# High and low parts of the normalised activations at another pair of places in most parts, in steps of 32 and 64 bytes

## The chip, the core and the metric

The kernel runs on one core of one Trainium2 chip. The metric is the device time of one execution in microseconds (us). Before the change it is 2287.13 us, the median of 3 runs (2279.85 to 2287.46).

## What is computed

The reference is a network of 4 layers over 256 tokens of 1024 features, in 32-bit floats. Each layer has three parts, each with a norm before and a norm after, so there are twelve parts, numbered 0 to 11 here (s in the code).

```python
for i in range(DEPTH):                                   # DEPTH = 4
    f = swiglu(rms_norm(x, norm_pre[i, 0]), w_gate, w_up, w_down)
    x = x + 0.5 * rms_norm(f, norm_post[i, 0])           # part 3i
    hn = rms_norm(x, norm_pre[i, 1])
    m = (dilated_attention, diff_attention, swa_sink_attention)[i % 3](hn, ...)
    x = x + rms_norm(m, norm_post[i, 1])                 # part 3i+1, "mixer"
    f = swiglu(rms_norm(x, norm_pre[i, 2]), ...)
    x = x + 0.5 * rms_norm(f, norm_post[i, 2])           # part 3i+2
```

So parts 0, 2, 3, 5, 6, 8, 9 and 11 are feed-forward parts with one shape (1024 to 2816 and back), parts 1 and 10 are the same dilated attention with other weights, part 4 is the differential attention, and part 7 the attention with a window and sinks.

## The kernel before

Every matrix product is computed as three matmuls on numbers that are split into a high and a low part: `mm3` (lines 173 to 176) issues high by high (line 174), high by low (175) and low by high (176) into one PSUM tile. The weights come from memory in units of 128x2048 numbers through `raw`; ScalarE rounds a unit to `hi` (line 141), and VectorE or GpSimd subtracts to get `lo` (line 142). `hi` and `lo` have four buffers each, and unit i, counted from the start of the program, uses buffer i mod 4. When a unit is used up, `done` starts the split of the unit four places later and a load behind that.

The normalised activations are transposed in `norm_tr_`: TensorE transposes four blocks into a PSUM bank, ScalarE rounds them into the high part of `xT` and VectorE subtracts to get the low part. `xT` is one tile of one buffer, made anew by `new_xT` at the first transposes of each part. It holds 2 x 2048 numbers and 64 more per partition; the high part begins 48 numbers (192 bytes) after the tile's start, and the low part 2048 numbers behind the high part.

In a feed-forward part (`ffn`) the first four units are used token by token: `xT` is the stationary operand, and the weights stream, 512 columns at a time, into `g` and `u` (48 matmuls each). The other 18 units are used feature by feature: the weights are stationary, and `xT` streams, 256 columns at a time, into `gu`. These are 18 x 48 = 864 matmuls in each of the eight feed-forward parts, in pairs of a gate unit and an up unit. Behind the first gate unit stand eight transposes (line 372). In the end `closing` multiplies the result, `hT`, by 11 more units, 512 columns at a time, into `acc`. A feed-forward part uses 33 units.

A mixer uses `xT` in the same two ways: as the stationary operand in the leading units (`lead`) and for the values (`v`), and streamed for the queries and keys (`qk`). Between these stand the scores (`sc`), transposes and weighted sums of the heads. Parts 1 and 10 use 44 units, part 4 uses 16 and part 7 uses 9. The result, `oT`, is multiplied in `closing` as well. `hT` and `oT` have places of their own, which the change doesn't touch.

TensorE's order is the program's order. Each matmul is a weight load (PEld in the profile) and a stream (PE); the load of the next matmul runs while the present one streams.

Of the kernel before, what the change touches and what calls it, by code (L numbers as in the profile page):

```python
# [45 lines left out]
def tile_network(  # L46
# [35 lines left out]
    def bank(tag, name):  # L82
        return ps.tile([P, 512], F32, tag=tag, name=name, bufs={"mm": 3, "s": 2, "tr": 2, "o": 1}[tag])
# [111 lines left out]
    xT = {}  # L195

    NX, NH = KD * SEQ, KF * SEQ

    def two(z, o, n):

        return [z[:, o + i * n:o + (i + 1) * n].rearrange("p (k n) -> p k n", n=SEQ) for i in range(2)]

    def new_xT():
        z = actp.tile([P, 2 * NX + 64], F32R, tag="xT", name="xT")
        xT["h"], xT["l"] = two(z, 48, NX)

    def xt(k, t):
        sl = slice(t * P, (t + 1) * P) if t is not None else slice(0, SEQ)
# [2 lines left out]
    def rstd_of(a, b, whole=False):  # L211

        ms = small.tile([P, 1], F32, tag="ms", name="ms")
        if whole:
            pool.tensor_scalar(out=ms, in0=a, scalar1=b, scalar2=None, op0=ALU.add)
        elif b is None:
            pool.tensor_scalar(out=ms, in0=a, scalar1=EPS, scalar2=None, op0=ALU.add)
        else:
            pool.tensor_scalar(out=ms, in0=a, scalar1=b, scalar2=EPS, op0=ALU.add, op1=ALU.add)  # L219
        r = small.tile([P, 1], F32, tag="rstd", name="rstd")  # L220
        state["rstd"] = pool.tensor_tensor(out=r, in0=ms, in1=half, op=ALU.pow).ins
        return r

    hn_of = {}

    def norm_elem(t, s, parts=1):

        ss = small.tile([P, 1], F32, tag="ssx", name="ssx")
        hn = actp.tile([P, D], F32, tag="w", name="hn", bufs=3)
        act.activation(out=hn, in_=x[:, t], func=AF.Square, scale=1.0 / 32.0, accum_out=ss)  # L230
        r = rstd_of(ss, None)
        state["norm"] = state["rstd"]
        for c in range(parts):
            cs = slice(c * D // parts, (c + 1) * D // parts)
            i = dve.scalar_tensor_tensor(out=hn[:, cs], in0=x[:, t, cs], scalar=r, in1=gains["pre", s][:, cs],
                                     op0=ALU.mult, op1=ALU.mult)
        hn_of[t] = hn
        return i

    def boundary_elem(t, s, acc, mid):  # L240
# [4 lines left out]
    def boundary_elem_(t, s, acc):  # L245

        ss = small.tile([P, 2], F32, tag="ssf", name="ssf")
        for i in range(2):
            act.activation(out=junk, in_=acc[i], func=AF.Square, scale=1.0 / 32.0,  # L249
                           accum_out=ss[:, i:i + 1])  # L250
        u = actp.tile([P, 2, 512], F32, tag="w", name="u", bufs=3)
        fac = 1.0 if s % 3 == 1 else 0.5
        g = gains["post", s].rearrange("p (i n) -> p i n", i=2)
        for i in range(2):
            dve.scalar_tensor_tensor(out=u[:, i], in0=acc[i], scalar=fac, in1=g[:, i],
                                     op0=ALU.mult, op1=ALU.mult)
        r = rstd_of(ss[:, 0:1], ss[:, 1:2])
        if s + 1 < 3 * DEPTH:
            dve.scalar_tensor_tensor(out=x[:, t], in0=u.rearrange("p i n -> p (i n)"), scalar=r,
                                     in1=x[:, t], op0=ALU.mult, op1=ALU.add)  # L260
            norm_elem(t, s + 1)
            return
        for i in range(2):
            cs = slice(i * 512, (i + 1) * 512)
            dve.scalar_tensor_tensor(out=x[:, t, cs], in0=u[:, i], scalar=r, in1=x[:, t, cs],
                                     op0=ALU.mult, op1=ALU.add)
            nc.sync.dma_start(out=out[:, t, cs], in_=x[:, t, cs])

    def norm_tr(t):
        with tc.high_priority(PR2) if t == 0 else ExitStack():  # L270
            return norm_tr_(t)

    def norm_tr_(t):
        hn = hn_of.pop(t)
        if t == 0:
            new_xT()
        for g in range(2):
            tp = bank("tr", "tp")
            for j in range(4):
                k = 4 * g + j  # L280
                pe.transpose(tp[:, j * P:(j + 1) * P], hn[:, k * P:(k + 1) * P], ident)
            tv = tp.rearrange("p (i n) -> p i n", i=4)
            h = xT["h"][:, 4 * g:4 * g + 4, t * P:(t + 1) * P]
            i = act.copy(out=h, in_=tv)
            dve.tensor_tensor(out=xT["l"][:, 4 * g:4 * g + 4, t * P:(t + 1) * P], in0=tv,
                              in1=h.bitcast(F32), op=ALU.subtract)
        return i
# [716 lines left out]
    if True:  # L1004
# [10 lines left out]
        with tc.high_priority(PRI):  # L1015
            i = norm_elem(0, 0, 2)
            j = norm_tr(0)
# [3 lines left out]
        with tc.issue_after(j.ins):  # L1021
            norm_elem(1, 0)
# [156 lines left out]
```

## Time and profile before

| | before |
|---|---|
| median of 3 runs | 2287.13 us |
| the profiled execution's own time | 2287.67 us |
| its span | 2285.8 us |
| TensorE, matmuls | 99% busy, 15,696 of them |
| TensorE, weight loads | 92% |
| VectorE, ScalarE, GpSimd | 55%, 52%, 28% |
| packets of the loads from memory, share of 16 DMA engines | 48.3% |

The busy time of TensorE is made of matmuls that overlap: a new one starts before the last one has drained. A matmul of 256 columns has a record of some 0.28 us, while the next starts 0.11 to 0.12 us later. So the share of busy time doesn't tell at what rate TensorE works. The rate is read from the starts in the timeline, or from the length of a stretch over the number of its matmuls.

### The profile page before, as it was taken

The page shows a single profiled execution, that of the slowest core. Times are in us where ns is not written, and L with a number is a line of the kernel's source. Part 1 is how long each engine was busy: PE and PEld are TensorE (multiplying, and loading weights), DVE is VectorE, ACT ScalarE, POOL GpSimd, SP SyncE. Part 2 cuts the span into 40 slices and gives each one's busy share as a digit, 9 for nine tenths or more (in the row PEclk, how much of TensorE's full clock was granted, in tenths as well). Part 3 has the DMA queues.
Part 4 walks back from the last instruction along what each step waited for, and adds up shares of the span by engine and source line. Part 5 has one row for each costly group of instructions (what it writes and reads, how often), then busy time and mean ns, then how long its engine had stood idle before and what let it go on. Part 6 is the DMA issues. An engine that isn't in the chain of part 4 may idle for free.

```text
span 2285.8 us, 38031 instructions
## 1 busy us (share of the span) xinstructions
PE 2253.5 (99%) x15696; PEld 2097.1 (92%) x15696; DVE 1253.8 (55%) x1814; ACT 1195.0 (52%) x2086; POOL 633.7 (28%) x640
## 2 busy tenths in 40 slices
PE   8999999999999999999999999999999999999998
PEld 7989999989989989889889987899899899998997
DVE  6555544565555555565465558654655544446653
ACT  6445666654444446654354448543444476665542
POOL 0005877620020028620020024100200287774000
PEclk9999999999999999999999999999999999999999
DMA  7554444445545545255555542555555544443552
GB/s 289 194 189 174 166 153 153 157 184 185 185 173 217 201 164 172 93 218 187 185 202 189 199 169 93 188 200 187 202 185 191 189 168 149 146 157 138 217 189 92
DMA packets 60519, 404.99 MB, mean 177 GB/s; under 512 B 6966, under 2 KB 7867, under 8 KB 16315
## 3 DMA queue, kind: packets, MB, share of 16 engines
q1 hardware_dynamic: 60202, 402.51, 48.3%
q8 instruction: 123, 2.02, 0.3%
q14 instruction: 50, 0.40, 0.1%
q10 hardware_dynamic: 144, 0.07, 0.0%
HBM read 401.50 MB, written 1.05 MB: 176 GB/s over the span
## 4 chain that ended last, share of the span: by engine, by line
PE 91%; DVE 4%; ACT 2%; POOL 2%; DMA 1%; issue 1%; SPq 0%; POOLq 0%; DVEq 0%; ACTq 0%
PE gu L175 12%; PE gu L174 12%; PE gu L176 12%; PE acc L176 8%; PE acc L174 8%; PE acc L175 8%; PE qk L174 4%; PE qk L175 4%; PE qk L176 4%; PE v L174 2%; PE v L175 2%; PE v L176 2%; PE tp L813 2%; DVE lo L142 1%; PE u L176 1%; PE u L175 1%
## 5 line engine op out<-in xcount | busy, mean ns | idle before, releaser
L141 ACT CAST hi<-raw 128x1024 fp32r<-128x1024 f32 (+2 forms) x970 | 775.1, 844 | 772.5 <-issue 492.9
L142 DVE TENSOR_TENSOR lo<-raw,hi 128x1024 fp32r<-128x1024 f32 (+1 forms) x546 | 661.6, 1250 | 422.6 <-ACT hi L141 422.2
L174 PE MATMUL gu<-xT,hi 128*128 128x256 f32 x2304 | 640.8, 278 | 0.0
L175 PE MATMUL gu<-xT,hi 128*128 128x256 f32 x2304 | 640.1, 278 | 0.0
L176 PE MATMUL gu<-xT,lo 128*128 128x256 f32 x2304 | 640.0, 278 | 0.0
L142 POOL TENSOR_TENSOR lo<-raw,hi 128x512 fp32r<-128x512 f32 (+1 forms) x424 | 546.5, 1322 | 146.3 <-ACT hi L141 146.0
L174 PEld LDWEIGHTS gu<-xT,hi 128*128 128x128 f32 x2304 | 436.0, 189 | 0.3
L175 PEld LDWEIGHTS gu<-xT,hi 128*128 128x128 f32 x2304 | 432.6, 188 | 0.4
L176 PEld LDWEIGHTS gu<-xT,lo 128*128 128x128 f32 x2304 | 432.5, 188 | 0.0
L219 POOL TENSOR_SCALAR ms<-ssf 128x1 f32<-128x1 f32 x24 | 7.2, 300 | 1393.0 <-ACT junk L249 1392.0
L176 PE MATMUL acc<-hi,hT 128*128 128x512 f32 x704 | 276.0, 392 | 0.0
L175 PE MATMUL acc<-lo,hT 128*128 128x512 f32 x704 | 275.9, 392 | 0.0
L174 PE MATMUL acc<-hi,hT 128*128 128x512 f32 x704 | 274.6, 390 | 0.0
L174 PE MATMUL qk<-xT,hi 128*128 128x256 f32 x800 | 226.1, 283 | 0.0
L176 PE MATMUL qk<-xT,lo 128*128 128x256 f32 x800 | 223.2, 279 | 0.0
L175 PE MATMUL qk<-xT,hi 128*128 128x256 f32 x800 | 223.2, 279 | 0.0
L175 PEld LDWEIGHTS acc<-lo,hT 128*128 128x128 f32 x704 | 132.2, 188 | 28.1
L176 PEld LDWEIGHTS acc<-hi,hT 128*128 128x128 f32 x704 | 132.2, 188 | 28.1
L174 PEld LDWEIGHTS acc<-hi,hT 128*128 128x128 f32 x704 | 132.3, 188 | 26.4
L174 PEld LDWEIGHTS qk<-xT,hi 128*128 128x128 f32 x800 | 151.6, 190 | 0.2
L176 PEld LDWEIGHTS qk<-xT,lo 128*128 128x128 f32 x800 | 151.0, 189 | 0.1
L175 PEld LDWEIGHTS qk<-xT,hi 128*128 128x128 f32 x800 | 150.8, 189 | 0.2
(267 smaller groups left out, 3298.2 us busy)
## 6 DMA issues: line engine op xcount, KB each, us to landing
raw<-in_w_ffn_dram SPq DMA_DIRECT2D x263, 1024.0 KB, 4.8
raw<-in_w_a_qk_dram SPq DMA_DIRECT2D x48, 1024.0 KB, 4.8
raw<-in_w_a_v_dram SPq DMA_DIRECT2D x32, 768.0 KB, 4.3
raw<-in_w_a_out_dram SPq DMA_DIRECT2D x8, 1024.0 KB, 4.8
raw<-in_w_b_qk_dram SPq DMA_DIRECT2D x8, 1024.0 KB, 5.2
gain<-in_g_pre_dram SPq DMA_DIRECT2D x12, 512.0 KB, 6.3
gain<-in_g_post_dram SPq DMA_DIRECT2D x12, 512.0 KB, 7.1
raw<-in_w_b_v_dram SPq DMA_DIRECT2D x4, 1024.0 KB, 4.7
```

The lines of the kernel that those rows point to most:

```text
L141: act.copy(out=hi[:, cs], in_=r[:, cs])
L142: eng.tensor_tensor(out=lo[:, cs], in0=r[:, cs], in1=hi[:, cs].bitcast(F32), op=ALU.subtract)
L174: pe.matmul(o, lhsT=a[0], rhs=b[0], start=first, stop=False)
L175: pe.matmul(o, lhsT=a[0], rhs=b[1], start=False, stop=False)
L176: pe.matmul(o, lhsT=a[1], rhs=b[0], start=False, stop=last)
L219: pool.tensor_scalar(out=ms, in0=a, scalar1=b, scalar2=EPS, op0=ALU.add, op1=ALU.add)
L813: pe.transpose(tp[:, c0:c0 + P], src, ident)
```

## The change

`new_xT` is told the part's number, and takes the places of the high and the low part from a table with a pair for each part. The first number of a pair is the place of the high part, in numbers of 4 bytes from the tile's start, the second that of the low part, less 2048. Before, both were 48 in all parts. Parts 0, 3 and 10 keep (48, 48). The tile has the same size and place as before, and every engine has the same instructions in the same order with the same waits; only the addresses in `xT` differ, of its two writers (ScalarE and VectorE) and its reader (TensorE).

| part | kind | high, low | in bytes, against before |
|---|---|---|---|
| 1 | mixer | 48, 64 | 0, +64 |
| 2 | feed-forward | 32, 48 | -64, 0 |
| 4 | mixer | 32, 64 | -64, +64 |
| 5 | feed-forward | 16, 48 | -128, 0 |
| 6 | feed-forward | 16, 64 | -128, +64 |
| 7 | mixer | 48, 56 | 0, +32 |
| 8 | feed-forward | 40, 48 | -32, 0 |
| 9 | feed-forward | 40, 40 | -32, -32 |
| 11 | feed-forward | 56, 56 | +32, +32 |

```diff
-    def new_xT():
+    def new_xT(s):
         z = actp.tile([P, 2 * NX + 64], F32R, tag="xT", name="xT")
-        xT["h"], xT["l"] = two(z, 48, NX)
+        a, b = ((48, 48), (48, 64), (32, 48), (48, 48), (32, 64), (16, 48), (16, 64), (48, 56), (40, 48),
+                (40, 40), (48, 48), (56, 56))[s]
+        xT["h"] = two(z, a, NX)[0]
+        xT["l"] = two(z, b, NX)[1]
...
-        hn_of[t] = hn
+        hn_of[t] = hn, s
...
-        hn = hn_of.pop(t)
+        hn, s = hn_of.pop(t)
         if t == 0:
-            new_xT()
+            new_xT(s)
```

## Rows read from the trace of the kernel before

**Rows 1.** The page: span, granted clock in 40 slices, chain by engine.

```profile
span 2285.8 us, 38031 instructions
...
PEclk9999999999999999999999999999999999999999
...
PE 91%; DVE 4%; ACT 2%; POOL 2%; DMA 1%; issue 1%; SPq 0%; POOLq 0%; DVEq 0%; ACTq 0%
```

**Rows 2.** Stretches of `gu`: from:to, length, busy (matmuls), clock, DMA share, GB/s.

```profile
36.10:135.00 98.90, 98.24 (x864) 1.00 0.57 205
500.70:603.10 102.40, 101.77 (x864) 1.00 0.54 197
687.80:786.60 98.80, 98.17 (x864) 1.00 0.56 204
1003.70:1106.10 102.40, 101.77 (x864) 1.00 0.54 196
1190.70:1289.60 98.90, 98.25 (x864) 1.00 0.56 203
1468.50:1567.30 98.80, 98.17 (x864) 1.00 0.55 203
1651.90:1754.40 102.50, 101.84 (x864) 1.00 0.54 196
2120.10:2219.00 98.90, 98.24 (x864) 1.00 0.56 205
```

**Rows 3.** Timeline of TensorE, part 3, behind the transposes: start, us, instruction.

```profile
694.03 0.37 PE L174 MATMUL gu<-xT,hi 128*128 128x256 f32 x1
...
694.47 0.28 PE L174 MATMUL gu<-xT,hi 128*128 128x256 f32 x1
...
694.92 0.28 PE L175 MATMUL gu<-xT,hi 128*128 128x256 f32 x1
```

**Rows 4.** Timeline of TensorE at the same place of part 2.

```profile
506.95 0.36 PE L174 MATMUL gu<-xT,hi 128*128 128x256 f32 x1
...
507.39 0.28 PE L174 MATMUL gu<-xT,hi 128*128 128x256 f32 x1
...
507.86 0.28 PE L175 MATMUL gu<-xT,hi 128*128 128x256 f32 x1
```

**Rows 5.** Tile views, `gu` (part 0, end of part 2), `qk` (part 1): ns min/median/max.

```profile
L175 PE MATMUL gu<-xT,hi x288: 276/276/282, 36.3 to 134.7; 128*128 128x256 f32 x144
...
L175 PE MATMUL gu<-xT,hi x10: 281/281/281, 599.7 to 602.9; 128*128 128x256 f32 x10
...
L175 PE MATMUL qk<-xT,hi x352: 276/280/282, 218.0 to 432.4; 128*128 128x256 f32 x176
```

**Rows 6.** Timeline of TensorE: `lead` of part 1, `g` and `u` of part 2.

```profile
212.26 0.28 PE L175 MATMUL lead<-lo,xT 128*128 128x256 f32 x1
...
217.21 0.28 PE L175 MATMUL lead<-lo,xT 128*128 128x256 f32 x1
...
490.40 0.39 PE L174 MATMUL g<-hi,xT 128*128 128x512 f32 x1
...
500.01 0.39 PE L174 MATMUL u<-hi,xT 128*128 128x512 f32 x1
```

**Rows 7.** Timeline of TensorE: `closing` of part 2, scores of part 1.

```profile
606.13 0.39 PE L175 MATMUL acc<-lo,hT 128*128 128x512 f32 x1
...
609.99 0.39 PE L174 MATMUL acc<-hi,hT 128*128 128x512 f32 x1
...
233.09 0.28 PE L174 MATMUL sc<-dg01h,qgh 128*128 128x256 f32 x1
...
233.45 0.28 PE L174 MATMUL qk<-xT,hi 128*128 128x256 f32 x1
```

**Rows 8.** Tile views, ScalarE: casts into `xT` and into `hT`, ns min/median/max.

```profile
L284 ACT CAST xT<-tp x48: 578/587/609, 10.9 to 2108.0; 128x512 fp32r<-128x512 f32 x48
...
L375 ACT CAST hT<-tp x16: 577/588/603, 44.1 to 2128.5; 128x512 fp32r<-128x512 f32 x16
```

## The prediction

> **What bounds the kernel now.** First the page: TensorE holds 91% of the chain of work that ended last, and its granted clock stands in the top tenth in all 40 slices [rows 1], which is the upper of its two levels, 2.4 GHz. So the end is set by the rate at which matmuls follow each other, and a gain has to come out of their spacing. Then the stretches of `gu`, the same 864 matmuls in each of eight parts. They come out at two lengths and nothing between: 98.2 us in parts 0, 3, 6, 8 and 11, and 101.8 us in parts 2, 5 and 9 [rows 2], with the same clock of 1.00 and nearly the same DMA share. Over 864 that is a spacing of 98.17 / 864 = 113.6 ns and 101.77 / 864 = 117.8 ns, 4.2 ns apart. Then the timeline at the place where the two part. Behind the eight transposes both parts begin alike, with a first matmul of 0.36 to 0.37 us and three steps that take 0.44 us in both. Then part 3 goes on with four steps in 694.92 - 694.47 = 0.45 us, or 0.113 us each [rows 3], part 2 with four in 507.86 - 507.39 = 0.47 us, or 0.118 us [rows 4], and each stays so for the rest of the stretch: the record of a matmul is 276 ns in the parts with the tight spacing and 281 ns in those with the wide one, with next to no spread [rows 5].
>
> So there are two steady spacings, tight and wide, and what starts them is small. What tells the parts apart? The instructions, waits and places of `xT` are the same in all eight. The buffers of the weights are not: a unit uses buffer i mod 4, and with 33 units in a feed-forward part and 44, 16 and 9 in the mixers the eight parts begin at units 0, 77, 110, 159, 192, 234, 267 and 344. The three that begin at an odd number, 77, 159 and 267, are parts 2, 5 and 9, those with the wide spacing: a match in eight out of eight. In these the gate units stand in the buffers where the other parts have their up units. I read this as the stream's place in SBUF against that of the weights which load meanwhile: an argument from a match, not a proof. The change moves one of the two sides.
>
> 113.6 ns looks like the floor of this operation. The closing matmuls, 512 columns on other tiles, follow at (609.99 - 606.13) / 17 = 227.1 ns [rows 7], twice 113.5, and no stretch of 256 columns that I found goes below 113 ns.
>
> **The change, term by term.** The sum is made against the profiled execution's 2287.67 us (span 2285.8 [rows 1] and 1.9 around it), which lies 0.5 above the median of 2287.13.
>
> `gu` of parts 2, 5 and 9 (moved, wide): 101.77 + 101.77 + 101.84 = 305.38 us. At the floor, with the mean of the five tight parts of 98.21, they would take 3 x 98.21 = 294.64. Between the bounds 0 and -10.74 I take **-10.7**, since the spacing that more parts show is the tight one, and the wide one has been seen in `gu` only with a pairing that goes away here.
>
> `gu` of parts 6, 8 and 11 (moved, tight): they can't fall below the floor, and can be thrown into the wide spacing, at 3 x (101.79 - 98.21) = +10.7. Between 0 and +10.7 I take **0**, by the rows they show now. Parts 0 and 3 are not moved: 0.
>
> `qk` of part 1 (1,056 matmuls; only the low part moves): a median of 280 ns on one of its lines, between the two records, with a smallest of 276 [rows 5], says that about half of them have the wide spacing. From half to none is 1,056 x 0.5 x 4.2 ns = -2.2 us; if three quarters of the matmuls have it and all lose it, -3.3; if the tight half turns wide, +2.2. I take **-2.2**, by the same reasoning as for `gu`. The few `qk` of parts 4 and 7 go with the next term.
>
> Token by token, where `xT` is the load and the weights stream: `g` and `u` in six moved parts (576), `lead` in parts 1, 4 and 7 (536) and `v` in parts 1 and 4 (480). `lead` runs at (217.21 - 212.26) / 42 = 117.9 ns and `g` and `u` at (500.01 - 490.40) / 42 = 228.8 ns [rows 6]. Against 113.6 and 227.1 that leaves at most 536 x 4.3 + 576 x 1.7 + 480 x 4.3 (`v` priced as `lead`) = 5.3 us. The other way, the widest steady spacing at hand, 0.36 / 3 = 120 ns in the scores [rows 7], would cost 1,592 x 2.1 ns = +3.3. I take a third of the gain, **-1.8**, since no second level is seen there.
>
> The writers of `xT`: the casts take a median of 587 ns into `xT`, and 588 ns into `hT` from the same bank, at another place [rows 8]. So a place costs them nothing, and 48 of them would be 0.5 us at 10 ns each: **0**. If TensorE takes less time, the loads and splits behind it must keep up: the tight parts already live with that at 0.55 to 0.57 of the DMA engines [rows 2], so nothing new is late.
>
> Sum: 2287.67 - 10.7 - 2.2 - 1.8 = **2273.0 us**.
>
> **A rule that speaks against it.** Two spacings of one instruction stream stand in the stretches of `gu` [rows 2], and they differ by what is read from where. The Trainium skill, "SBUF — State Buffer", section "Who interferes with whom", says that TensorE has two read ports of its own, for the stream and for the weights, and never waits on anyone; its specifications put the lines of SBUF at 16 bytes, so that steps of 32 and 64 bytes leave a stream's place in a line as it was. By that page no place is better than another, and the sum would be 2287 us. The trace doesn't settle it, since no run here has `xT` elsewhere; but a rule by which places are all alike has no room for the odd and the even parts.
>
> **The rivals.** (1) A new draw: the place decides, but as by lot. Five of eight parts are tight now. Drawn so, the three wide parts gain 3 x 5/8 x 3.6 = 6.7 us and the three tight ones lose 3 x 3/8 x 3.6 = 4.0, net -2.7; with half of the smaller terms (-2.0) that is 2283 us, anywhere from 2276 to 2290. For it: mixers, with many restarts, mix both records in one line [rows 5]. Against: a new place was hardly needed where a part is tight. (2) Nothing happens: the spacing is set by the timing behind the transposes and not by the place, and the change does nothing that can be measured: 2287 us. For it: the two entries differ by hundredths of a us [rows 3, 4]. Against: the odd and even units. The page of the Trainium skill named above would give this time for another reason. (3) Slower than before: the new places throw the quick `gu` of parts 6, 8 and 11 into the wide spacing, while parts 2, 5 and 9 keep theirs, as a larger distance to the weights' buffers makes the streams meet more often. The price is +10.7, and with the token-by-token matmuls at 120 ns (+3.3) the time is 2301.7 us. It decides from the point where two more parts are lost than won. For it: `lead` reads the same two tiles in exchanged roles and shows the wide spacing alone [rows 6]. Against: five tight parts out of eight.
>
> **How the numbers follow.** My forecast has a chance of 0.55, rival 1 has 0.25, rival 2 has 0.13 and rival 3 has 0.07. About 0.5%, 11.4 us, is what a measurement of this kernel can tell from no change; so under 2275.7 is faster and over 2298.6 slower. The forecast lies on the faster side by 2.7 us only: a little of it (two of three wide parts won) falls to the same, and rival 1 gives as much back at its good end. So faster 0.55, same 0.38, slower 0.07. The range: all bounds on the good side give 2287.67 - 10.7 - 3.3 - 5.3 = 2268.4, and one of the runs before lies 7.3 below the median, twice 3.6, as if two parts had changed their spacing in it; I go to 2264. On the other side it takes in rivals 1 and 2, to 2288. Left out are rival 3 and the ends, under 0.2 in all.
>
> **What would show it.** The stretches of `gu` in parts 2, 5 and 9 at 98.2 us and not 101.8 prove the main term; each that stays costs 3.6. The same stretches in parts 6, 8 and 11 at 98.2 prove the second, at 101.8 rival 3. `qk` of part 1 with a median of 276 to 277 on all three lines proves the third, and `lead` under 117.9 or `u` under 228.8 the fourth. All eight stretches as before would be rival 2. Parts 0, 3 and 10, not moved, must stay; if part 3 or 10 changes, timing has a hand in it. A spacing under 113 ns would show that my floor is none, and the time could then fall below the range.

## The result: 2307.86 us, slower by 0.9%

The changed kernel takes 2307.86 us, the median of 4 runs (2305.27 to 2313.5), against 2287.3 us before (4 runs). The ratio is 1.0091, with a 95% interval of 1.0073 to 1.0109. I had forecast 2273.0 us, a gain of 0.6%, with a range of 2264 to 2288. The time lies 20 us above the range and on the other side of no change.

The page of the changed kernel shows the same picture as before: the same instructions, TensorE at the head of the chain, the clock at its upper level.

```profile
span 2307.1 us, 38031 instructions
...
PEclk9999999999999999999999999999999999999999
...
PE 90%; DVE 4%; POOL 3%; ACT 2%; DMA 1%; issue 1%; SPq 0%; POOLq 0%; DVEq 0%; ACTq 0%
```

The stretches of `gu`, in the order of parts 0, 2, 3, 5, 6, 8, 9, 11 (columns as in [rows 2]):

```profile
35.70:134.50 98.80, 98.16 (x864) 1.00 0.57 204
503.80:609.30 105.50, 104.83 (x864) 1.00 0.53 191
693.90:792.80 98.90, 98.25 (x864) 1.00 0.56 203
1009.90:1112.60 102.70, 102.05 (x864) 1.00 0.55 196
1197.40:1301.00 103.60, 102.94 (x864) 1.00 0.53 193
1480.10:1582.80 102.70, 102.05 (x864) 1.00 0.54 196
1667.70:1771.10 103.40, 102.77 (x864) 1.00 0.53 194
2137.20:2240.30 103.10, 102.47 (x864) 1.00 0.54 196
```

Put beside [rows 2], parts 0 and 3, which are not moved, stand at 98.2 us as before. All six moved parts lie at 102 us or over: part 6 rose by 4.7 us, 8 by 3.9, 11 by 4.2, and of the three that I had hoped to win back part 2 rose by 3.1, 5 by 0.3 and 9 by 0.9. The sum is +17.1 us of the 21.3 by which the span grew. `qk` of part 1 (all 1,056 matmuls) now takes 132.80 us, against 129.96 before, while part 10 with the same shape and the old pair takes 129.96 in both kernels. In order: part 1 before, part 1 after, part 10 after:

```profile
195.00:477.60 282.60, 129.96 (x1056) 1.00 0.44 159
...
195.00:480.40 285.40, 132.80 (x1056) 1.00 0.43 157
...
1831.00:2113.70 282.70, 129.96 (x1056) 1.00 0.45 159
```

In that stretch of part 1 no line of `qk` reaches the record of 276 ns any more, which was the smallest in [rows 5], and the median is 281 ns on all three. One of them (ns min/median/max):

```profile
L175 PE MATMUL qk<-xT,hi x352: 277/281/285, 217.6 to 435.0; 128*128 128x256 f32 x176
```

Token by token, `g` and `u` of part 2 follow at (497.08 - 494.74) / 10 = 234 ns, against 228.8 in [rows 6]:

```profile
494.74 0.40 PE L174 MATMUL g<-hi,xT 128*128 128x512 f32 x1
...
497.08 0.39 PE L175 MATMUL g<-lo,xT 128*128 128x512 f32 x1
```

So 17.1 us are from `gu`, 2.8 from `qk` of part 1, and most of the rest from `g` and `u`. In these stretches TensorE doesn't sit idle: each matmul of a moved part follows its predecessor by a few ns more.

How far the spacing went is seen best behind the transposes. The 80 us from 1020 to 1100 lie there in part 5 in both kernels; the first line is before, the second after:

```profile
1020.00:1100.00 80.00, 80.00 (x682) 1.00 0.53 186
...
1020.00:1100.00 80.00, 80.00 (x682) 1.00 0.52 185
```

The same 682 matmuls: part 5 goes on at the wide spacing that it had, 117.8 ns, and most of its 0.3 us more lies in the unit ahead of the transposes, which was tight before. Part 8 fell from the tight spacing to this same wide one. The other four moved parts are wider still, from 118.3 ns in part 11 to 121 in part 2.

### The profile page after: what moved, and what is told of

It reads as the page before. It is cut to its first block, busy times and chain, and to the rows that moved or that the text cites. A ratio compares the mean times of both kernels' runs of the same rounds, so it can differ in the third digit from the quotient of the medians.

```text
span 2307.1 us, 38031 instructions
## 1 busy us (share of the span) xinstructions
PE 2275.5 (99%) x15696; PEld 2117.3 (92%) x15696; DVE 1252.6 (54%) x1814; ACT 1194.4 (52%) x2086; POOL 633.0 (27%) x640
## 4 chain that ended last, share of the span: by engine, by line
PE 90%; DVE 4%; POOL 3%; ACT 2%; DMA 1%; issue 1%; SPq 0%; POOLq 0%; DVEq 0%; ACTq 0%
PE gu L175 12%; PE gu L176 12%; PE gu L174 12%; PE acc L174 8%; PE acc L176 8%; PE acc L175 7%; PE qk L174 4%; PE qk L175 4%; PE qk L176 4%; PE v L176 2%; PE v L175 2%; PE v L174 2%; POOL lo L142 2%; PE tp L816 1%; PE u L176 1%; PE u L174 1%
```

## The experiments

Three things had to be told apart: whether the place or the entry sets the spacing, against what the place counts, and whether anything moved can reach the tight spacing. All kernels compute the whole network. Each was timed and traced in one execution, except where a median is given. The fences of this section show stretches of `gu`, with the columns of [rows 2].

**Three parts back.** The changed kernel's table with three pairs undone:

```diff
-        ... (16, 48), (16, 64), (48, 56), (40, 48), (40, 40), (48, 48), (56, 56))[s]
+        ... (16, 48), (48, 48), (48, 56), (48, 48), (40, 40), (48, 48), (48, 48))[s]
```

> The changed kernel, with parts 6, 8 and 11 put back to the pair (48, 48). Theory A, the spacing of a part's matmuls is set by the places of its own xT against the buffers of the weights: the three stretches of gu go from 102.9, 102.1 and 102.5 us back to 98.2, the other parts stay to 0.1 us (part 2 at 104.8, part 9 at 102.8), and with the token-by-token matmuls (some 0.5 us a part) the time is 2309 - 13 - 1.5 = 2294.5 us. Theory B, the spacing is set by the timing with which a stretch is entered: parts that are not edited here change as well, by 3.6 us or more each, and the sum does not come out.

It took 2297.61 us, 3 us over the sum of theory A. Parts 2, 6, 8 and 11:

```profile
505.00:607.90 102.90, 102.13 (x864) 1.00 0.55 195
1195.70:1294.80 99.10, 98.35 (x864) 1.00 0.58 203
1473.40:1576.00 102.60, 101.88 (x864) 1.00 0.55 196
2130.00:2229.00 99.00, 98.27 (x864) 1.00 0.58 203
```

Parts 6 and 11 came back, as A says. Part 8 came back to (48, 48) and to its other spacing, the wide one that it did not have before. And part 2, which was not edited here, fell from 104.8 to 102.1 us. So neither theory does alone: the pair sets which spacings a part can have, and something else picks one of them.

**The buffers of the weights turned.** One buffer is passed over at the start, all pairs (48, 48):

```diff
+        if i == 0:
+            for tag in ("hi", "lo"):
+                z = wp.tile([P, 2048], F32R, tag=tag, name=tag)
+                pool.memset(z[:, :1].bitcast(F32), 0.0)
         hi = wp.tile([P, 2048], F32R, tag="hi", name="hi")
```

> The kernel before, with one set of the weights' four buffers passed over at the start, so that every unit of weights stands one buffer further; all pairs (48, 48). Theory A, in the form that the match of odd and even units suggests (which buffer a unit stands in matters): the stretches of gu of parts 2, 5 and 9 go from 101.8 to 98.2 us, and those of parts 0, 3, 6, 8 and 11 from 98.2 to 101.8, +7.2 us in all, 2295 us. Theory B (timing at the entry): no swap, the eight stretches stay as they are or change without a pattern. If only the place within 256 bytes counts, the buffers are alike, nothing changes, and the time is 2287 us.

It took 2285.01 us. Parts 2, 5, 6 and 9:

```profile
501.40:600.50 99.10, 98.37 (x864) 1.00 0.57 203
...
1000.80:1099.90 99.10, 98.37 (x864) 1.00 0.57 203
1184.20:1286.80 102.60, 101.87 (x864) 1.00 0.55 196
...
1649.20:1751.80 102.60, 101.90 (x864) 1.00 0.55 197
```

No swap: parts 6 and 9 are wide, all others tight. The match of odd units and wide parts, on which I had built, does not hold.

**Before, once more.** The same program in another execution.

> The kernel before once more, in an execution of its own. If the entry timing picks between the two spacings that (48, 48) allows, and differs from execution to execution, other parts than 2, 5 and 9 lie at 101.8 us, and the time is 2276.5 us + 3.6 for each part that does (three: 2287). If it is fixed by the program, the same three parts lie there and the time is 2287 us.

It took 2285.65 us. Parts 2, 5, 6 and 9:

```profile
501.10:603.70 102.60, 101.85 (x864) 1.00 0.55 196
...
1003.70:1102.70 99.00, 98.28 (x864) 1.00 0.57 203
1187.10:1289.70 102.60, 101.85 (x864) 1.00 0.54 196
...
1653.40:1752.50 99.10, 98.33 (x864) 1.00 0.57 203
```

Parts 2 and 6 are wide here, where it was 2, 5 and 9 [rows 2]. With (48, 48) the level of a part changes from execution to execution, as in a draw. The eight out of eight of my prediction were a coincidence in one trace. Counted over the traces of all 13 kernels, 45 of the 60 stretches with `xT` at the old distance from the weights (or 256 bytes further, see below) are tight behind the transposes, and none of the 44 at other distances.

**High and low part moved together.**

```diff
+        a, b = ((48, 48), (48, 48), (16, 16), (0, 0), (48, 48), (32, 32), (16, 16), (48, 48), (32, 32), (64, 64), (48, 48), (64, 64))[s]
```

> The kernel before, with the high and the low part moved together, 2048 numbers apart as before: parts 2 and 6 at 16, 3 at 0, 5 and 8 at 32, 9 and 11 at 64, the others at 48. If the distance between the high and the low part is what counts (theory C), all of them stay at 98.2 or 101.8 us. If the distance to the weights' buffers counts (theory A), the moved parts leave these two levels, as parts 9 and 11 did in the changed kernel with 40 and 56 (102.8 and 102.5 us), and 0 and 64, a multiple of 256 bytes apart, come out alike. By A the time is 2287 + 4 x 4 (parts 3, 6, 8, 11) + 1 x 3 = 2306 us, by C 2287.

It took 2314.01 us. Parts 2 (16), 3 (0), 5 (32), 6 (16), 8 (32), 9 and 11 (64):

```profile
501.10:603.90 102.80, 102.04 (x864) 1.00 0.55 196
688.20:792.90 104.70, 103.98 (x864) 1.00 0.54 194
1009.90:1113.50 103.60, 102.86 (x864) 1.00 0.55 195
1198.30:1301.20 102.90, 102.17 (x864) 1.00 0.54 195
1481.60:1586.30 104.70, 103.99 (x864) 1.00 0.53 193
1670.50:1775.30 104.80, 104.03 (x864) 1.00 0.54 194
2140.70:2245.40 104.70, 103.97 (x864) 1.00 0.54 194
```

Theory C, the distance between high and low part, fails. No moved part is tight, though A went too far in having them leave both levels: at 16 the spacing behind the transposes is 117.8 ns, the wide level itself. 0 and 64, 256 bytes apart, give the same 104.0 us three times; 16 gives 102.1 twice; 32 has two spacings, 102.9 and 104.0. The time is 8 us over what A had as its estimate, since I had put 4 us on a part and it is up to 5.8.

**Everything moved together.** 64 bytes stand in front of all buffers:

```diff
     half = const.tile([P, 1], F32, name="half")
+    gap = const.tile([P, 16], F32, name="gap")
```

> The kernel before, with 64 bytes put in front of all buffers, so that xT and the weights move together; all pairs (48, 48). Theory A (the distance between xT and the weights' buffers): the eight stretches of gu stay at 98.2 and 101.8 us, and the time is 2287 us. If the place of xT by itself counts (its high part would begin where a pair of 64 puts it), the stretches change like those of the moved parts in the changed kernel, by +0.3 to +4.8 us each, 2300 us or more.

It took 2280.3 us; parts 0 and 2:

```profile
36.50:139.30 102.80, 102.09 (x864) 1.00 0.56 197
504.60:603.60 99.00, 98.32 (x864) 1.00 0.57 203
```

The other six lie at 98.25 to 98.33. Part 0 is wide from the start: its unit ahead of the transposes already follows at 117.8 ns. `xT` now starts where a pair of 64 would put it, and 64 alone gave 104.0 in each of its parts. So not the place counts but the distance: `xT` and the weights may move by 64 bytes if they move together.

**The low weights moved alone, and with the low part.** `lo` stands 64 bytes further, and a second gap of 192 bytes puts all behind it back modulo 256 bytes:

```diff
+        if i == 0:
+            z = wp.tile([P, 16], F32, tag="gap", name="gap", bufs=1)
+            ...
         lo = wp.tile([P, 2048], F32R, tag="lo", name="lo")
+        if i == 0:
+            z = wp.tile([P, 48], F32, tag="gap2", name="gap2", bufs=1)
+            ...
```

> The kernel before, with the four lo buffers of the weights 64 bytes further, all else at the same place modulo 256 bytes; the low part of xT follows them by 64 bytes, pair (48, 64), in parts 3, 6, 9 and 11, and stays, (48, 48), in parts 0, 2, 5 and 8. Theory D, what counts is the place of the stream against the weights that load while it runs (high part against hi, low part against lo): where both moved, the distances are those of before, and gu takes 98.2 or 101.8 us, mostly 98.2; where lo moved alone, it takes neither, but 102 to 105 us. Theory E, what counts is the stream against the weights that it is multiplied by, or the distance between the high and the low part: the four parts with (48, 64) lie at 102 to 105 us, and by the distance of the two parts alone the four with (48, 48) keep 98.2. The time itself says little, since the closing matmuls read lo too.

It took 2328.04 us. Parts 2 and 3:

```profile
509.80:613.00 103.20, 102.46 (x864) 1.00 0.54 196
699.00:802.40 103.40, 102.72 (x864) 1.00 0.55 195
```

All four parts with (48, 48) lie at 102.5, all four with (48, 64) at 102.7. Moving `lo` alone loses the tight spacing, though nothing in `xT` moved: the weights are one side of it. Moving the low part along does not bring it back, so theory D falls as I had put it. E had two forms. The distance between the high and the low part falls too, since by it the four parts with (48, 48) would have kept 98.2 us; the stream against the weights that it is multiplied by fits both halves. The closing matmuls, which stream `lo`, became wider too, as expected.

**One of the two alone.** The low part by 64 bytes in parts 2 and 3 and by 32 in 5 and 6; the high part by -64, -32 and -128 in 8, 9 and 11:

```diff
+        a, b = ((48, 48), (48, 48), (48, 64), (48, 64), (48, 48), (48, 56), (48, 56), (48, 48), (32, 48), (40, 48), (48, 48), (16, 48))[s]
```

> The kernel before, with one of the two parts of xT moved: the low part by 64 bytes in parts 2 and 3, by 32 in 5 and 6; the high part by -64 in part 8, by -32 in 9, by -128 in 11. Theory D: each of the two distances is enough to spoil the tight spacing, so all seven lie at 101.8 us or over (part 8 at 102.0 or 104.8, the two that the pair (32, 48) has shown, part 9 near 102.1, part 11 near 102.1), and none at 98.2. If the high part alone counts, parts 2, 3, 5 and 6 lie at 98.2 or 101.8. Time by D: 2287 + 4 x 4 + 3 = 2306 us.

It took 2308.22 us. Parts 3, 6, 8 and 11:

```profile
688.10:790.90 102.80, 102.10 (x864) 1.00 0.55 197
...
1196.40:1300.20 103.80, 103.08 (x864) 1.00 0.54 193
1480.40:1583.40 103.00, 102.26 (x864) 1.00 0.54 196
...
2136.80:2239.60 102.80, 102.10 (x864) 1.00 0.54 197
```

None of the seven is tight: either part's place is enough to lose it.

**Small steps.** Parts 2 and 3 at 44, 5 and 6 at 46, 8 and 9 at 52, 11 at 50:

```diff
+        a, b = ((48, 48), (48, 48), (44, 44), (44, 44), (48, 48), (46, 46), (46, 46), (48, 48), (52, 52), (52, 52), (48, 48), (50, 50))[s]
```

> The kernel before, with the high and the low part moved together by 8 and 16 bytes: parts 2 and 3 at 44, 5 and 6 at 46, 8 and 9 at 52, 11 at 50, the others at 48. If the tight spacing belongs to a window around 48, the nearest pairs, 46 and 50, keep gu at 98.2 (or 101.8) us, and 44 and 52 lie between those and the 102 to 103 us of 40 and 56. If it belongs to 48 alone or to a place in steps of 32 bytes, all moved parts lie over 101.8. Time: 2287 + 4 x 4 at most for parts 3, 6, 8 and 11, so 2284 to 2303 us.

It took 2314.66 us, 12 us over the top of what I had expected. Parts 3 (44), 6 (46), 8 (52) and 11 (50):

```profile
689.00:793.00 104.00, 103.31 (x864) 1.00 0.55 194
...
1199.50:1304.20 104.70, 103.96 (x864) 1.00 0.53 192
1483.20:1587.10 103.90, 103.21 (x864) 1.00 0.55 194
...
2141.30:2246.00 104.70, 103.99 (x864) 1.00 0.54 193
```

There is no window around 48: 8 bytes to either side are among the worst places measured.

**256 bytes further.** All pairs (112, 112), with a tile that is longer by 64 numbers:

```diff
-        z = actp.tile([P, 2 * NX + 64], F32R, tag="xT", name="xT")
+        z = actp.tile([P, 2 * NX + 128], F32R, tag="xT", name="xT")
```

> The kernel before, with the high and the low part 256 bytes further in all parts, pair (112, 112), and the tile longer by as much. If the distance counts modulo 256 bytes, as 0 and 64 with the same 103.7 us suggest, all stretches of gu lie at 98.2 or 101.8 us, and the time is 2280 to 2288 us. If the place near the tile's start counts, the stretches lie over 101.8 and the time at 2310 us.

It took 2288.45 us, with five parts tight and three (3, 6 and 9) wide. Parts 2 and 3:

```profile
501.60:600.60 99.00, 98.25 (x864) 1.00 0.57 203
685.10:787.70 102.60, 101.91 (x864) 1.00 0.55 197
```

The levels of 48 are back, and no others: 256 bytes further is the same distance. Half of that isn't: the pair (16, 16) stands 128 bytes from (48, 48), and its two parts had lost the tight spacing. (What 0 and 64 had shown is 104.0 us, not 103.7.)

**The interruption put at the end.** The eight transposes go behind the last gate unit:

```diff
-            def up(sg, u):
-                h = fp.tile([P, 512], F32, tag="h", name="h")
+            def up(sg, u, tag="h"):
+                h = fp.tile([P, 512], F32, tag=tag, name="h")
...
-                hs[t] = up(sg, u)
+                hs[t] = up(sg, u, "h0")
...
-                        if c == 2:
+                        if c == 10:
                             transposes(0)
                             transposes(1)
```

> The kernel before, all pairs (48, 48), with the eight transposes of a feed-forward part put behind the last gate unit instead of the first (the two tiles that they read get buffers of their own). In every part and every run so far the 48 matmuls of gu ahead of the transposes followed at the tight spacing (5.5 us a unit), and what came behind them was tight or wide. If the interruption is what picks the spacing, 17 of the 18 units are tight in all eight parts: gu at 98.2 us, or 98.4 where the last unit is wide, and the time is 2276.5 us, with no spread by 3.6 us between executions, against 2284 to 2288 of before. If something else picks it, two to three parts still lie at 101.8 and the time is 2284 to 2288 us.

With the pairs of before it took 2277.97 us, the median of 9 runs that span 2277.15 to 2279.58. The kernel before, beside it, took 2285.89 us in 14 runs that span 2277.41 to 2292.17. The ratio is 0.9962, with a 95% interval of 0.9949 to 0.9976: this is the version that beats both kernels. Parts 2, 3 and 9:

```profile
501.40:600.50 99.10, 98.32 (x864) 1.00 0.59 207
684.90:784.10 99.20, 98.50 (x864) 1.00 0.58 207
...
1645.90:1745.10 99.20, 98.50 (x864) 1.00 0.57 207
```

All eight parts stand at 98.25 to 98.52 us. The three at 98.5 have the wide spacing in their last unit alone, behind the transposes. So the interruption is where the tight spacing gets lost. The spread of before, 15 us in 14 runs, fits the number of wide parts at 3.6 us each: the traced executions at the old distance took 2280.3 us with one wide part, 2285.01 and 2285.65 with two, 2287.67 and 2288.45 with three.

What I had put down for the unit ahead of the transposes was too wide: it is tight at the old distance (59 of 60 stretches), but at the others it follows at 116.7 to 121.1 ns. And which level comes behind the transposes can be read before them, from the records of the first three high-by-high matmuls (line 174). The kernel before, parts 2 (wide) and 3 (tight), ns min/median/max:

```profile
L174 PE MATMUL gu<-xT,hi x3: 276/279/279, 500.7 to 501.4; 128*128 128x256 f32 x3
...
L174 PE MATMUL gu<-xT,hi x3: 276/281/285, 687.8 to 688.5; 128*128 128x256 f32 x3
```

With part 0 and the kernel with everything moved left aside, the longest of the three is 279 ns in all 14 wide stretches at the old distance and 285 in all 27 tight ones, in this run too, where 17 units lie between. So the transposes don't draw by themselves: the stretch comes to them in one of two conditions. This is a sign and not the cause, since in the cases left aside 279 goes with tight as well.

**The same with the changed table.**

> The changed kernel with the same move of the transposes. If the moved pairs have no tight spacing at all, the stretches of gu stay at 102 to 105 us in the moved parts, and the time is 2305 us or more. If they have one, and are only thrown out of it by the transposes, they come down to 98.2 us and the time to 2282 us.

It took 2310.71 us, and parts 2 and 5 stand where they stood in the changed kernel:

```profile
505.00:610.50 105.50, 104.78 (x864) 1.00 0.54 195
1011.00:1113.80 102.80, 102.10 (x864) 1.00 0.56 200
```

The other four moved parts lie at 102.08 to 102.88. Without the interruption too the moved pairs don't come to the tight spacing. So the change didn't just draw badly: it took the tight spacing out of the draw.

## Why the prediction was wrong, step by step

- **What bounds the kernel** was right: the spacing of the matmuls, at two levels with (48, 48), 113.6 and 117.8 ns. That the places of `xT` against the weights matter was right as well: they decide whether the tight spacing can be had at all, which is now shown by three runs together: `xT` moved alone loses the tight spacing (104.0 us at 64), `lo` moved alone loses it (102.5), everything moved together keeps it (98.3).
- **`gu` of parts 2, 5 and 9, -10.7**: they came out at +4.3. This is the step that failed. I took the tight spacing as what a part falls into unless a bad pairing of buffers stops it, because five of eight parts had it. In fact it exists at the distance that the kernel had (and 256 bytes further), and in none of the 44 stretches at the others tried (0, 16, 32, 40, 44, 46, 50, 52, 56, 64 together, six pairs of unequal numbers in feed-forward parts, and `lo` moved). The three parts at 101.8 were unlucky draws at the best place tried.
- **`gu` of parts 6, 8 and 11, 0**: they came out at +12.8, over the bound of +10.7. The bound was wrong too: I had taken the two levels of one place for the only ones. Elsewhere there are more: in 14 of those 44 stretches the steady spacing is the old wide one of 117.8 ns, in the other 30 it lies between 118.2 and 121.1, up to 104.8 us in part 2.
- **The odd and even units** were the evidence for the first step, and fell in two runs. One trace gave one draw for each of eight parts; a match of eight with a property that I went looking for is weaker than it looks. The times before would have warned me: 2279.85 beside 2287.46 is a jump by two parts' worth in the same program. I saw it and put it into the range, not into the reasons.
- **`qk` of part 1, -2.2**: +2.8, for the same reason. A move of the low part alone was enough.
- **Token by token, -1.8**: `g` and `u` widened from 228.8 to 234 ns in part 2, while `lead` stayed near 118. The sign was wrong; by the busy time of the tiles in the moved parts, `g` and `u` grew by 1.8 us, `v` by 0.4 and `lead` by 0.2, together +2.4, within the bound of +3.3.
- **The writers, 0**: right. The casts into `xT` took a median of 586 ns, against 587 in [rows 8].
- **The rivals.** Rival 3 had the right sign, named the right parts for its price, and got 0.07. Its 2301.7 us is 6 short, as parts 2, 5 and 9 do not simply keep their level and the levels go higher than it had them. Its reason, streams that meet more often, is not shown by any run. Rival 1, a new draw, was the right picture for the place before and the wrong one for the new places. Rival 2 is out, since the place counts: 98.2 us at one and 104.0 at another for the same 864 matmuls. The Trainium skill, "SBUF — State Buffer", section "Who interferes with whom", has TensorE wait on no one, by which I had all places alike. The trace does not agree, with these two times.

**What stays open.** Which of the distances take the tight spacing away is not settled. There are four, of the high and the low part to `hi` and to `lo`, and no move changes one alone: the high part alone changes its two, the low part alone its two, `lo` alone its two, and `lo` with the low part those of high to `lo` and of low to `hi`. Each of these four moves lost the tight spacing, and no one distance changes in all four, so at least two count; `hi` was not moved alone. Nor do the runs show why the distance of the old place is the good one, or what puts a stretch into one of its two conditions before it begins.

## What to carry to other kernels

A place in SBUF that looks arbitrary, here 48 numbers, can be worth 0.9% where TensorE is the bound: look at the starts of long runs of equal matmuls, and if their spacing has levels, scan the places, all parts together, before moving any one. A level that differs between equal stages of one trace may be a draw; profile the same program twice before explaining it. Where a steady run is interrupted by other work, putting the interruption at its end was worth 0.4% here and took away most of the spread.

## What the runs showed that I had not expected

- The spacing of matmuls of 256 columns depends on the distance between the stream and the weights modulo 256 bytes: 113.6 ns or 117.8 at the old place, 103.98 / 864 = 120.3 ns at 0 and 64, and the old levels again 256 bytes further.
- It is sharp: 8 bytes off the good place cost 104.0 - 98.2 = 5.8 us in 864 matmuls.
- A steady spacing holds for a hundred us once it is there, and can change at an interruption by transposes, from execution to execution in other parts: the same program had parts 2, 5 and 9 wide once, and parts 2 and 6 the next time. The records of the first matmuls, 279 or 285 ns, told which it would be in 41 of 41 stretches, with part 0 and the kernel with everything moved left aside.
